# A fused decoder layer on one Trainium2 core: the second norm between the adaLN bursts, and small products stacked in the rounded format

## The chip, the cores and the metric

The kernel runs on one core of one Trainium2 chip. The metric is the device time of one execution in microseconds (us). The engines are named as in the profile: PE (TensorE matmul) with PEld (its weight loads), DVE (VectorE), ACT (ScalarE), POOL (GpSimd) and SP (SyncE, which issues most weight loads).

## The reference

One layer of a hybrid decoder is computed for two groups that share all weights: a prompt of 256 tokens and 8 sample sequences of 8 tokens, 320 token columns together. Everything is float32.

```python
mod = silu(c) @ w_ada + b_ada;  sh1, sc1, g1, sh2, sc2, g2 = split(mod, 6)
h = rmsnorm(x, norm1_g) * (1 + sc1) + sh1
q, k, v, og, u, ga, gb, alr = split(h @ w_in)            # alr: rank 16
loga = log_sigmoid(alr @ w_a2 + b_a) / 16                # gate logits
o, s_new = gla(q, k, v, loga, s0)                        # 4 heads, chunks of 16 tokens, masked
y_a = rmsnorm(o, gla_norm_g) * silu(og);  y_b = pool(u)
x = x + g1 * ((sigmoid(ga) * y_a + sigmoid(gb) * y_b) @ w_o)
h2 = rmsnorm(x, norm2_g) * (1 + sc2) + sh2
gate, up = split(h2 @ w_gu)
x = x + g2 * ((silu(gate) * up) @ w_down)
```

Model width is 2048, FFN width 5632, head sizes 256 (keys) and 512 (values). Outputs are the final normed tokens, the GLA states and the pooling buffers.

## The kernel before

Activations lie transposed, 128 features by 320 tokens a tile, 16 tiles for the model width. Weights stream from HBM in chunks of 0.5 MB. PE has a rounded format of float32 (fp32r), and each projection is built from three such products: a weight chunk is split by ACT into its rounded part whi (L147) and by DVE into the rest wlo (L148), activations are split in the same way into a high and a low tile (hh/hl after the first norm, mh/ml before w_o, h2h/h2l after the second norm), and `mm3` (L161 to L163) adds whi with high, whi with low and wlo with high. whi and wlo have four buffers each (WB = 4, 512 columns a buffer).

The order is: the first adaLN sections and norm; then, head by head, the projections of w_in (units q, k, u, v, og, ga, gb) with steps of GLA and of the pooling branch laid between them; then w_o (with the residual and the squares for each feature tile, L937 to L971); the second norm (L973 to L996); the FFN in two parts of 22 tiles each. A tile scheduler moves instructions within what dependences, buffers and its own estimate of times allow, so that the order on an engine isn't that of the code.

What the change touches:

- `alr_proj` (L462 to L479), once: the low-rank gate input. Two chunks of eight feature tiles; weights of 16 columns sit in 64-column tiles wal (whi and wlo kept apart), with three matmuls per feature tile, 48 in all.
- In `gla_steps`, one call a head: `s_wa2` (L540 to L544) loads w_a2 and b_a on POOL's queue; `s_gk` (L546 on) makes the gate logits by three full float32 matmuls (L549). `s_attP` computes the masked products of keys and queries of the sample sequences (four sequences of eight tokens to a 128 x 128 tile, two tiles gg), and `s_inter(gg)` multiplies them by the sample values vp, in full float32 (L736), and adds the product with the carried state (L740). The sample key tile keP holds two copies of its rows; the values vp stacked by rows serve the state update (L761) in the rounded format as well.
- `ada_burst` (L267 on): adaLN for the second half of the layer is computed in 30 bursts, each a group of matmuls (L279) on a piece of w_ada that `ada_load` and `ada_piece` have loaded (L255, POOL's queue). Bursts 24 and 25 (eight feature tiles each) finish the first half of section 5 (g2), 26 to 29 (four each) the second half. When a half is finished, its sums are copied from PSUM to adasb (ACT L286), transposed by PE (L125) and added to mod (DVE L291).
- At the second norm: bursts 24 and 25 and the norm's sum over partitions (L975) stand behind the last w_o matmul; from it come the root (ACT L977), the reciprocal (DVE L978), the products h (DVE L989, for the sample columns POOL L990 and L991), h2h (ACT L992, L993) and h2l (DVE L994, L996). The first unit of the FFN takes gate and up together. Bursts 26 to 29 stand in the FFN at f = 4, 8, 12 and 16.

Of the kernel before, what the change touches and what calls it, by code (L numbers as in the profile page):

```python
# [11 lines left out]
F32 = mybir.dt.float32  # L12
F32R = mybir.dt.float32r
# [7 lines left out]
P = 128  # L21
# [20 lines left out]
def shape_constants():  # L42
    s = np.arange(P)[:, None]
    c = np.arange(P)[None, :]
    m = 32 * (c // 32) + 15
    dq = ((s > m) & (s <= c)).astype(np.float32) - ((s > c) & (s <= m)).astype(np.float32)
    e = np.zeros((P, 4, 4), np.float32)
    for j in range(4):
        for i in range(j + 1, 4):
            sv = np.arange(P)  # L50
            e[:, j, i] = (sv > 32 * j + 15) & (sv <= 32 * i + 15)
    e = e.reshape(P, 16)
    after = (s > c).astype(np.float32)
# [12 lines left out]
    cf = np.concatenate([inv.reshape(P, 64), m0, m1, ms], 1).astype(np.float32)  # L66
    mask = (s <= c).astype(np.int32)
    r = np.arange(P)[:, None]
    q = np.arange(P)[None, :]
    mp = ((r // 32 == q // 32) & ((r % 32) < 16) & ((q % 32) < 8)  # L70
          & ((r % 8) <= (q % 32))).astype(np.int32)
# [5 lines left out]
CFW = NM0 + NM1 + NMS + 64  # L77


def body(tc, A):  # L80
# [22 lines left out]

    cst = cp.tile([P, 2 * P + 64], F32, name="cst")
# [4 lines left out]
    invc = cst[:, 2 * P:2 * P + 64]  # L109
    cumr = cp.tile([P, NM0 + NM1 + NMS], F32R, name="cumr")  # L110
    M0, M1, MS = cumr[:, 0:NM0], cumr[:, NM0:NM0 + NM1], cumr[:, NM0 + NM1:NM0 + NM1 + NMS]
# [8 lines left out]
    N1G, N2G, FG, PSC, GNG = vec[:, 0:16], vec[:, 16:32], vec[:, 32:48], vec[:, 48:64], vec[:, 64:68]  # L120
    alr = cp.tile([P, 3 * P], F32, name="alr")

# [119 lines left out]
    BURSTS += [(5, 0, 0, 8), (5, 0, 8, 8)] + [(5, NBA, k0, 4) for k0 in range(0, KT, 4)]  # L242
    AMIX, AEND = 24, 26
    ada_raw = {}
    ada_done = []
    ada_want = []
    ada_ps = []

    def ada_piece(after=None):
# [7 lines left out]
    def ada_load(n, bufs):  # L257

        if n < len(BURSTS) and n not in ada_raw:
            nk = BURSTS[n][3]  # L260
            t = ada_raw[n] = apool[0].tile([P, nk, NBA * P], F32, tag="big", bufs=bufs, name=nm("araw"))
            ada_want.extend((n, t, r) for r in range(0, nk, 2))
# [5 lines left out]
    def ada_burst():  # L268
# [7 lines left out]
        with tc.high_priority(), tc.issue_after(last_mm[0]):  # L276
            for r in range(nk):
                for j in range(4):
                    PE.matmul(ps[32 * j:32 * j + 32, 0:2 * P], lhsT=scT[:, k0 + r, :],  # L279
                              rhs=ada_raw[n][:, r, 2 * j * P:(2 * j + 2) * P],  # L280
                              start=k0 + r == 0, stop=k0 + r == KT - 1, tile_position=(0, 32 * j))
        if k0 + nk < KT:
# [109 lines left out]
    with tc.tile_pool(name="head", bufs=1) as xp:  # L392
# [69 lines left out]
        def alr_proj(walr, cum):  # L462
            V.tensor_copy(cumr, cum)
            pa = misc()
            for k0 in range(0, KT, 8):
                wal = []
                for tag in ("whi", "wlo"):
                    t = wp.tile([P, 8, 64], F32R, tag=tag, bufs=WB, name=nm("wal"))
                    G.memset(t.bitcast(F32), 0.0)
                    wal.append(t)  # L470
                wk = walr[:, k0:k0 + 8]
                S.copy(wal[0][:, :, 0:16], wk)
                V.tensor_sub(wal[1][:, :, 0:16], wk, wal[0][:, :, 0:16].bitcast(F32))
                for j in range(8):
                    k = k0 + j
                    mm3(pa[:64, 0:T], wal[0][:, j], wal[1][:, j], hh[k], hl[k], k == 0, k == KT - 1)
            G.memset(alr, 0.0)
            G.memset(alr[32:33, :], 1.0)
            V.tensor_copy(alr[0:16, 0:T], pa[0:16, 0:T])  # L479

        g0 = new_group(0)
        new_gates(g0)
        for si, (k0, k1) in enumerate(SLICES):
# [10 lines left out]
            elif si == len(SLICES) - 1:  # L494
# [3 lines left out]
                cum = xp.tile([P, NM0 + NM1 + NMS], F32, name="cum")  # L498
                nc.gpsimd.dma_start(cum, A["cf"][:, 64:CFW])
                nc.gpsimd.dma_start(invc, A["cf"][:, 0:64])  # L500
            us = units(0)
# [33 lines left out]
    def gla_steps(g):  # L535
# [4 lines left out]
        def s_wa2():  # L540
            wa2 = E["wa2"] = w4([P, DK])
            G.memset(wa2, 0.0)
            nc.gpsimd.dma_start(wa2[0:16, :], A["w_a2"][0, :, DK * h:DK * h + DK])
            nc.gpsimd.dma_start(wa2[32:33, :], A["b_a"][:, DK * h:DK * h + DK])  # L544

# [41 lines left out]
        def s_prod():  # L587
# [145 lines left out]
        def s_inter(gg):  # L733
            def f():
                pt = E["oi"] = misc()
                PE.matmul(pt, lhsT=attP[:, gg], rhs=E["vp"][:, gg].bitcast(F32), start=True, stop=False,  # L736
                          skip_group_check=True)
# [220 lines left out]

    ada_load(AMIX, 2)
    ada_load(AMIX + 1, 2)  # L960
    for ui in range(8):
# [11 lines left out]
    def rstd_bcast(acc):  # L973
        pt = misc()
        PE.matmul(pt[:, 0:T], lhsT=ones, rhs=acc, start=True, stop=True)  # L975
        rs = fp.tile([P, T], F32, tag="rs", name=nm("rs"))
# [5 lines left out]
    ada_burst()  # L982
    rs = rstd_bcast(acc)
    ada_burst()
    h2h = [hp.tile([P, T], F32R, tag="hh%d" % k, name="h2h%d" % k) for k in range(KT)]
# [20 lines left out]
    for pi, (f0, f1) in enumerate(parts):  # L1006
        ah, al = {}, {}
        for f in range(f0, f1, 2):
            sg = fa.tile([P, 2, T], F32, tag="sg", name=nm("sg"))
            if f == 0:  # L1010
                pg, pu = projs(((wgu, f * P), (wgu, FF + f * P)), 0, KT, h2h, h2l)
                S.activation(sg, pg[:, :, 0:T], AF.Silu)
# [10 lines left out]
            if pi == 0 and f >= 2:  # L1023
                if f in (4, 8, 12, 16):
                    ada_burst()
                if f in (2, 4, 8, 12):
                    ada_load(len(ada_done), 1)
                    ada_all()
# [70 lines left out]
```

## Time and profile before

| | |
|---|---|
| time, median of 3 runs | 1989.35 us (1987.7 to 1989.87) |
| profiled execution | 1987.48 us |
| its span | 1985.2 us |
| mean granted TensorE clock | 0.996 |
| busy: PE, PEld | 97%, 91% |
| busy: DVE, ACT, POOL | 50%, 41%, 9% |
| moved by DMA | 400.59 MB, mean 202 GB/s |

The span is the profiled part of one execution. A matmul's record shows when it starts and how long it is under way; in a steady stream the next starts before the last one's record ends, so the cost of a matmul is read from one start to the next. A full float32 matmul shows as two rows. "<-" in a row stands between the written and the read tiles, and a bracket at the end of a row gives the idle time of the engine ahead of it and what ended it.

### The profile page before, as it was taken

What the parts mean: (1) busy time and instruction counts of PE and PEld (TensorE: products, weight loads), DVE (VectorE), ACT (ScalarE), POOL (GpSimd) and SP (SyncE); (2) the same over time, 40 slices, a digit from 0 to 9 for tenths busy, and PEclk for the clock granted to TensorE, in tenths of its full rate; (3) what the DMA queues carried; (4) which work ended last, traced back from release to release, by engine and by line L of the source; (5) the groups of instructions that cost most, each with busy time, mean ns of one, the idle gap of its engine ahead of it and who ended that gap; (6) DMA issues with size and microseconds to landing.
All of it is one profiled execution on the core that took longest, in us unless ns stands there. A gap on an engine that the chain in (4) does not pass through costs nothing.

```text
span 1985.2 us, 34772 instructions
## 1 busy us (share of the span) xinstructions
PE 1934.8 (97%) x13888; PEld 1816.4 (91%) x13888; DVE 998.8 (50%) x1895; ACT 821.7 (41%) x1459; POOL 170.1 (9%) x292
## 2 busy tenths in 40 slices
PE   5999999999999999999999999999999999999997
PEld 3778998988898889989989999999999999999997
DVE  2655645655355535664565444444444444444554
ACT  3323633643345333553444333333333434344443
POOL 1002102211111111111130000000000000000000
PEclk9999999999999999999999999999999999999998
DMA  9997458659865777479745555444444444444443
GB/s 317 349 332 245 133 170 283 231 191 326 292 193 185 277 270 246 147 251 328 271 139 160 184 189 178 155 145 144 156 147 151 149 154 151 150 149 141 148 142 101
DMA packets 309275, 400.59 MB, mean 202 GB/s; under 512 B 12417, under 2 KB 273057, under 8 KB 308777
## 3 DMA queue, kind: packets, MB, share of 16 engines
q1 hardware_dynamic: 279754, 291.17, 45.8%
q0 software_dynamic: 29360, 107.21, 14.7%
q8 instruction: 108, 1.77, 0.4%
q14 instruction: 53, 0.43, 0.1%
HBM read 373.90 MB, written 24.67 MB: 201 GB/s over the span
## 4 chain that ended last, share of the span: by engine, by line
PE 75%; DMA 2%; issue 1%; POOL 1%; ACT 0%; DVE 0%; ACTq 0%; POOLq 0%
PE ps L161 23%; PE ps L163 23%; PE ps L162 23%; PE pm L279 3%; DMA araw<-w_ada 2%; PE pm L125 1%; PE pm L740 0%; PE pm L761 0%; PE pm L709 0%; DMA o_gs<-S 0%; PE pm L736 0%; POOL og L382 0%; PE pm L698 0%; PE psy L161 0%; PE pm L575 0%
## 5 line engine op out<-in xcount | busy, mean ns | idle before, releaser
L148 DVE TENSOR_TENSOR wlo<-raw,whi 128x512 fp32r<-128x512 f32 x952 | 655.2, 692 | 785.9 <-ACT whi L147 780.4
L147 ACT CAST whi<-raw 128x512 fp32r<-128x512 f32 x952 | 586.2, 622 | 940.1 <-PE ps L162 860.9
L161 PE MATMUL ps<-hh,whi 128*128 128x320 f32 x1408 | 442.5, 315 | 2.2 <-ACT whi L147 1.1
L161 PE MATMUL ps<-h2h,whi 128*128 128x320 f32 x1408 | 435.5, 309 | 4.9 <-ACT h2h L993 4.9
L162 PE MATMUL ps<-hl,whi 128*128 128x320 f32 x1408 | 439.1, 312 | 0.0
L163 PE MATMUL ps<-hh,wlo 128*128 128x320 f32 x1408 | 436.6, 313 | 1.4 <-DVE wlo L148 1.3
L162 PE MATMUL ps<-h2l,whi 128*128 128x320 f32 x1408 | 435.0, 309 | 0.0
L163 PE MATMUL ps<-h2h,wlo 128*128 128x320 f32 x1408 | 434.7, 309 | 0.0
L161 PEld LDWEIGHTS ps<-hh,whi 128*128 128x128 f32 x1408 | 264.3, 188 | 25.0 <-issue 13.3
L163 PEld LDWEIGHTS ps<-hh,wlo 128*128 128x128 f32 x1408 | 263.6, 188 | 17.6 <-issue 8.6
L162 PEld LDWEIGHTS ps<-hl,whi 128*128 128x128 f32 x1408 | 264.5, 188 | 7.5 <-issue 6.4
L161 PEld LDWEIGHTS ps<-h2h,whi 128*128 128x128 f32 x1408 | 264.9, 188 | 6.8 <-ACT h2h L993 5.2
L162 PEld LDWEIGHTS ps<-h2l,whi 128*128 128x128 f32 x1408 | 264.8, 188 | 0.0
L163 PEld LDWEIGHTS ps<-h2h,wlo 128*128 128x128 f32 x1408 | 264.7, 188 | 0.1
L161 PE MATMUL ps<-ah,whi 128*128 128x320 f32 x704 | 217.7, 309 | 0.0
L162 PE MATMUL ps<-al,whi 128*128 128x320 f32 x704 | 216.5, 308 | 0.0
L163 PE MATMUL ps<-ah,wlo 128*128 128x320 f32 x704 | 216.5, 308 | 0.0
L162 PEld LDWEIGHTS ps<-al,whi 128*128 128x128 f32 x704 | 131.9, 187 | 0.0
L161 PEld LDWEIGHTS ps<-ah,whi 128*128 128x128 f32 x704 | 131.9, 187 | 0.0
L163 PEld LDWEIGHTS ps<-ah,wlo 128*128 128x128 f32 x704 | 131.9, 187 | 0.0
L255 POOL DMA_DIRECT2D araw<-w_ada x64 | 45.9, 719 | 441.5 <-PE pm L279 423.3
L163 PE MATMUL ps<-mh,wlo 128*128 128x320 f32 x256 | 79.6, 311 | 0.0
(279 smaller groups left out, 1580.9 us busy)
## 6 DMA issues: line engine op xcount, KB each, us to landing
raw<-w_gu SPq DMA_DIRECT2D x176, 512.0 KB, 3.5
raw<-w_in SPq DMA_DIRECT2D x173, 512.0 KB, 4.3
araw<-w_ada POOLq DMA_DIRECT2D x64, 1024.0 KB, 7.7
raw<-w_down SPq DMA_DIRECT2D x80, 512.0 KB, 3.4
raw<-w_ada SPq DMA_DIRECT2D x64, 512.0 KB, 6.9
S<-state_gla POOLq DMA_DIRECT2D x16, 1024.0 KB, 9.1
o_gs<-S POOLq DMA_DIRECT2D x16, 1024.0 KB, 5.8
raw<-w_o SPq DMA_DIRECT2D x32, 512.0 KB, 4.9
```

Of the source, the lines that this page charges most:

```text
L125: PE.transpose(out, in_, ident[:k, :k])
L147: S.copy(hi, raw)
L148: V.tensor_sub(lo, raw, hi.bitcast(F32))
L161: PE.matmul(ps, lhsT=whi, rhs=xhi, start=start, stop=False)
L162: PE.matmul(ps, lhsT=whi, rhs=xlo, start=False, stop=False)
L163: last_mm[:] = [PE.matmul(ps, lhsT=wlo, rhs=xhi, start=False, stop=stop).ins]
L255: nc.gpsimd.dma_start(t[:, r:r + 2], wada[:, k0 + r:k0 + r + 2, col:col + NBA * P])
L279: PE.matmul(ps[32 * j:32 * j + 32, 0:2 * P], lhsT=scT[:, k0 + r, :], rhs=ada_raw[n][:, r, 2 * j * P:(2 * j + 2) * P], start=k0 + r == 0, s ...
```

## The change

Four parts of the kernel change:

1. The weights of the low-rank projection are stacked in one 128-column tile: rounded part and rest in 32 columns, three times. Two matmuls per feature tile (with hh and with hl) give all products at once, 32 in all. `alr` becomes a tile in the rounded format whose rows hold high and low parts, by one subtraction with a column of minus ones and zeros (TAKE_A).
2. `s_wa2` loads six copies of w_a2 and two of b_a and splits them by rows in the same way (an ACT cast and a DVE scalar_tensor_tensor), so the three matmuls of `s_gk` are in the rounded format.
3. keP holds four copies, the mask keeps the rows of the copies, and a cast and a scalar_tensor_tensor turn attP into attR, whose rows hold high and low parts; `s_inter` uses it in the rounded format.
4. The norm's sum over partitions stands between bursts 24 and 25, burst 26 follows, and the first FFN unit is issued behind the last matmul of burst 26. Burst 26 is loaded during w_o, and the FFN keeps the bursts 27 to 29, at f = 4, 8 and 12.

The core of the diff:

```diff
-            for k0 in range(0, KT, 8):
...
-                    mm3(pa[:64, 0:T], wal[0][:, j], wal[1][:, j], hh[k], hl[k], k == 0, k == KT - 1)
-            G.memset(alr, 0.0)
-            G.memset(alr[32:33, :], 1.0)
-            V.tensor_copy(alr[0:16, 0:T], pa[0:16, 0:T])
+            for k0 in range(0, KT, 4):
+                t = wp.tile([P, 4, P], F32R, tag="whi", bufs=WB, name=nm("wal"))
+                G.memset(t[:, :, 96:P].bitcast(F32), 0.0)
+                wk = walr[:, k0:k0 + 4]
+                S.copy(t[:, :, 0:16], wk)
+                V.tensor_sub(t[:, :, 16:32], wk, t[:, :, 0:16].bitcast(F32))
+                G.tensor_copy(t[:, :, 32:64], t[:, :, 0:32].bitcast(F32))
+                G.tensor_copy(t[:, :, 64:96], t[:, :, 0:32].bitcast(F32))
+                for j in range(4):
+                    k = k0 + j
+                    PE.matmul(pa[:, 0:T], lhsT=t[:, j], rhs=hh[k], start=k == 0, stop=False)
+                    PE.matmul(pa[:, 0:T], lhsT=t[:, j], rhs=hl[k], start=False, stop=k == KT - 1)
+            ah_ = xp.tile([P, T], F32R, name="alrh")
+            S.copy(ah_, pa[:, 0:T])
+            V.scalar_tensor_tensor(alr[:, 0:T], ah_.bitcast(F32), TAKE_A, pa[:, 0:T], op0=ALU.mult, op1=ALU.add)
...
         def s_wa2():
-            wa2 = E["wa2"] = w4([P, DK])
-            G.memset(wa2, 0.0)
-            nc.gpsimd.dma_start(wa2[0:16, :], A["w_a2"][0, :, DK * h:DK * h + DK])
-            nc.gpsimd.dma_start(wa2[32:33, :], A["b_a"][:, DK * h:DK * h + DK])
+            raw = w4([P, DK])
+            G.memset(raw, 0.0)
+            for r in range(0, 96, 16):
+                nc.gpsimd.dma_start(raw[r:r + 16, :], A["w_a2"][0, :, DK * h:DK * h + DK])
+            for r in (96, 97):
+                nc.gpsimd.dma_start(raw[r:r + 1, :], A["b_a"][:, DK * h:DK * h + DK])
+            hi = w4([P, DK], F32R)
+            S.copy(hi, raw)
+            wa2 = E["wa2"] = w4([P, DK], F32R)
+            V.scalar_tensor_tensor(wa2, hi.bitcast(F32), TAKE_W, raw, op0=ALU.mult, op1=ALU.add)
...
+                G.tensor_copy(keP[:, d, :, 2 * LS:4 * LS], keP[:, d, :, 0:2 * LS])
...
+            hi = w4([P, 2, P], F32R)
+            S.copy(hi, attP)
+            E["attR"] = lp.tile([P, 2, P], F32R, tag="attR", name=nm("attR"))
+            V.scalar_tensor_tensor(E["attR"], hi.bitcast(F32), TAKE_T, attP, op0=ALU.mult, op1=ALU.add)
...
-                PE.matmul(pt, lhsT=attP[:, gg], rhs=E["vp"][:, gg].bitcast(F32), start=True, stop=False,
+                PE.matmul(pt, lhsT=E["attR"][:, gg], rhs=E["vp"][:, gg], start=True, stop=False,
...
-    ada_load(AMIX, 2)
-    ada_load(AMIX + 1, 2)
+    for n in range(AMIX, AMIX + 3):
+        ada_load(n, 2)
...
-        PE.matmul(pt[:, 0:T], lhsT=ones, rhs=acc, start=True, stop=True)
+        last_mm[:] = [PE.matmul(pt[:, 0:T], lhsT=ones, rhs=acc, start=True, stop=True).ins]
...
     ada_burst()
     rs = rstd_bcast(acc)
+    ada_burst()
     ada_burst()
...
-                pg, pu = projs(((wgu, f * P), (wgu, FF + f * P)), 0, KT, h2h, h2l)
+                with tc.issue_after(last_ada[0]):
+                    pg, pu = projs(((wgu, f * P), (wgu, FF + f * P)), 0, KT, h2h, h2l)
...
-                if f in (4, 8, 12, 16):
+                if f in (4, 8, 12):
                     ada_burst()
-                if f in (2, 4, 8, 12):
+                if f in (2, 4, 8):
```

What the scheduler makes of it is seen in the order of the instructions on each engine. PE at the second norm, before: the last w_o matmul (ps, mh), the two bursts (araw), the sum over partitions (acc) and the transposes (adasb), then the first gate unit.

```order
L163 MATMUL ps_10614<-mh_9440,wlo_10738 128x320
L279 MATMUL pm_10769<-araw_9520,scT 32x256 x32
L279 MATMUL pm_10769<-araw_9521,scT 32x256 x32
L975 MATMUL pm_10802<-acc_9517,cst 128x320
L125 MATMUL pm_10839<-cst,adasb_10840 128x128 x2
L161 MATMUL ps_11014<-h2h_10845,whi_11018 128x320
```

The same place after the change (lines are those of the changed kernel):

```order
L167 MATMUL ps_10679<-mh_9502,wlo_10803 128x320
L284 MATMUL pm_10834<-araw_9582,scT 32x256 x32
L993 MATMUL pm_10867<-acc_9579,cst 128x320
L284 MATMUL pm_10834<-araw_9583,scT 32x256 x32
L129 MATMUL pm_10904<-cst,adasb_10905 128x128
L284 MATMUL pm_10910<-araw_9584,scT 32x256 x16
L129 MATMUL pm_10904<-cst,adasb_10905 128x128
L165 MATMUL ps_11096<-h2h_10927,whi_11100 128x320
```

The sum over partitions moved ahead of the second burst, and a third burst stands between the two transposes, ahead of the first gate matmul.

ACT at the same place, before: the last squares, the copy of the burst's sums, the root, then the high parts h2h of 256 prompt columns and 64 sample columns.

```order
L940 ACTIVATE sq_10765<-x_15_9516 128x320
L286 COPY adasb_10840<-pm_10769 128x256
L977 ACTIVATE rs_10804<-pm_10802,epst 128x320
L992 ACTIVATE h2h_10845<-h_1755_10877,mod 128x256
L992 ACTIVATE h2h_10846<-h_1756_10885,mod 128x256
L993 CAST h2h_10845<-h_1755_10877 128x64
```

And after the change:

```order
L958 ACTIVATE sq_10830<-x_15_9578 128x320
L995 ACTIVATE rs_10869<-pm_10867,epst 128x320
L1011 ACTIVATE h2h_10927<-h_1773_10959,mod 128x256
L1011 ACTIVATE h2h_10928<-h_1774_10967,mod 128x256
L1012 CAST h2h_10927<-h_1773_10959 128x64
L291 COPY adasb_10905<-pm_10834 128x256
L1011 ACTIVATE h2h_10929<-h_1775_10975,mod 128x256
```

The copy to adasb moved from ahead of the root to behind the first cast of 64 sample columns.

POOL in the first head after the change, with what each instruction waits for (DMASW0 to DMASW7 are the eight lanes of its DMA queue): the loads of `s_wa2`, between a clearing of the raw tile and a product of the og gate. Before, one load of w_a and one of b_a stood there.

```order
L549 MEMSET w_455_2689 128x256
L823 MEMSET u_2760 128x2x15 [waits DVE_49,Pool_49]
L551 DMA w_455_2689<-w_a 16x256 [waits DMASW4_49,Pool_49]
L551 DMA w_455_2689<-w_a 16x256 [waits DMASW5_49]
L551 DMA w_455_2689<-w_a 16x256 [waits DMASW6_49]
L551 DMA w_455_2689<-w_a 16x256 [waits DMASW7_49]
L551 DMA w_455_2689<-w_a 16x256 [waits DMASW0_49]
L551 DMA w_455_2689<-w_a 16x256 [waits DMASW1_49]
L553 DMA w_455_2689<-b_a 1x16x16 [waits DMASW2_49]
L553 DMA w_455_2689<-b_a 1x16x16 [waits DMASW3_49]
L387 TENSOR_TENSOR og_264<-og_264,sg_3005 128x640 [waits Activation_49]
```

The two loads became eight, each behind the transfer that its lane carried last.

PE in the last head, where the sum over partitions of the head's norm (acc) stands; before, among projections over hh:

```order
L161 MATMUL ps_9217<-hh_87,whi_9236 128x320
L162 MATMUL ps_9217<-hl_103,whi_9236 128x320
L777 MATMUL pm_8452<-acc_8445,cst 128x320
L279 MATMUL pm_8881<-araw_7942,scT 32x256 x16
L163 MATMUL ps_9217<-hh_87,wlo_9237 128x320
```

After the change it stands among the products of the pooling branch (psy), with 16 of them still to come:

```order
L165 MATMUL psy_9439<-dh_8178,whi_9459 128x320
L166 MATMUL psy_9439<-dl_8179,whi_9459 128x320
L795 MATMUL pm_8514<-acc_8507,cst 128x320
L284 MATMUL pm_8943<-araw_7988,scT 32x256 x16
L165 MATMUL psy_9440<-dh_8178,whi_9443 128x320
```

It moved from a place with 82 projection matmuls over hh and 24 of psy behind it in the head to one behind which the products for w_o follow soon.

More of the change, by code (lines that the diff above doesn't have):

```diff
@@ L65, in shape_constants @@
         inv[:, g] = (1.0 / np.minimum(np.arange(16) + 1, w).astype(np.float32))[None]
-    cf = np.concatenate([inv.reshape(P, 64), m0, m1, ms], 1).astype(np.float32)
+    r = np.arange(P)
+    take = -1.0 * np.stack([(r // 32 == 2) | (r == 97), r // 32 == 1, r % 32 >= 16], 1)
+    cf = np.concatenate([inv.reshape(P, 64), take, m0, m1, ms], 1).astype(np.float32)
     mask = (s <= c).astype(np.int32)
@@ L69, in shape_constants @@
     q = np.arange(P)[None, :]
-    mp = ((r // 32 == q // 32) & ((r % 32) < 16) & ((q % 32) < 8)
+    mp = ((r // 32 == q // 32) & ((q % 32) < 8)
           & ((r % 8) <= (q % 32))).astype(np.int32)
@@ L76 @@
 NM0, NM1, NMS = 272, 400, 128
-CFW = NM0 + NM1 + NMS + 64
+CFC = 64 + 3
+CFW = NM0 + NM1 + NMS + CFC
 def body(tc, A):
@@ L101, in body @@
     V, S, G, PE = nc.vector, nc.scalar, nc.gpsimd, nc.tensor
-    cst = cp.tile([P, 2 * P + 64], F32, name="cst")
+    cst = cp.tile([P, 2 * P + CFC], F32, name="cst")
     msk = cp.tile([P, 2 * P], I32, name="msk")
@@ L109, in body @@
     invc = cst[:, 2 * P:2 * P + 64]
+    TAKE_W, TAKE_A, TAKE_T = (cst[:, 2 * P + 64 + i:2 * P + 65 + i] for i in range(3))
     cumr = cp.tile([P, NM0 + NM1 + NMS], F32R, name="cumr")
@@ L120, in body @@
     N1G, N2G, FG, PSC, GNG = vec[:, 0:16], vec[:, 16:32], vec[:, 32:48], vec[:, 48:64], vec[:, 64:68]
-    alr = cp.tile([P, 3 * P], F32, name="alr")
+    alr = cp.tile([P, 3 * P], F32R, name="alr")
     def tr(out, in_):
@@ L242, in body @@
     BURSTS += [(5, 0, 0, 8), (5, 0, 8, 8)] + [(5, NBA, k0, 4) for k0 in range(0, KT, 4)]
-    AMIX, AEND = 24, 26
+    AMIX = 24
     ada_raw = {}
@@ L247, in body @@
     ada_ps = []
+    last_ada = []
     def ada_piece(after=None):
@@ L260, in ada_load @@
             nk = BURSTS[n][3]
-            t = ada_raw[n] = apool[0].tile([P, nk, NBA * P], F32, tag="big", bufs=bufs, name=nm("araw"))
+            t = ada_raw[n] = apool[0].tile([P, nk, NBA * P], F32, tag="big" if nk == 4 else "big2", bufs=bufs if nk == 8 else 1, name=nm("araw"))
             ada_want.extend((n, t, r) for r in range(0, nk, 2))
@@ L278, in ada_burst @@
                 for j in range(4):
-                    PE.matmul(ps[32 * j:32 * j + 32, 0:2 * P], lhsT=scT[:, k0 + r, :],
-                              rhs=ada_raw[n][:, r, 2 * j * P:(2 * j + 2) * P],
-                              start=k0 + r == 0, stop=k0 + r == KT - 1, tile_position=(0, 32 * j))
+                    last_ada[:] = [PE.matmul(ps[32 * j:32 * j + 32, 0:2 * P], lhsT=scT[:, k0 + r, :],
+                                             rhs=ada_raw[n][:, r, 2 * j * P:(2 * j + 2) * P],
+                                             start=k0 + r == 0, stop=k0 + r == KT - 1, tile_position=(0, 32 * j)).ins]
         if k0 + nk < KT:
@@ L464, in alr_proj @@
             pa = misc()
-            for k0 in range(0, KT, 8):
[L466 to L474, printed above, removed]
-                    k = k0 + j
-                    mm3(pa[:64, 0:T], wal[0][:, j], wal[1][:, j], hh[k], hl[k], k == 0, k == KT - 1)
-            G.memset(alr, 0.0)
-            G.memset(alr[32:33, :], 1.0)
-            V.tensor_copy(alr[0:16, 0:T], pa[0:16, 0:T])
+            for k0 in range(0, KT, 4):
[7 more added lines that the diff above has]
+                for j in range(4):
+                    k = k0 + j
+                    PE.matmul(pa[:, 0:T], lhsT=t[:, j], rhs=hh[k], start=k == 0, stop=False)
[3 more added lines that the diff above has]
+            V.scalar_tensor_tensor(alr[:, 0:T], ah_.bitcast(F32), TAKE_A, pa[:, 0:T], op0=ALU.mult, op1=ALU.add)
+            G.memset(alr[:, T:3 * P].bitcast(F32), 0.0)
+            G.memset(alr[96:98, :].bitcast(F32), 1.0)
         g0 = new_group(0)
@@ L498, in body @@
                 cum = xp.tile([P, NM0 + NM1 + NMS], F32, name="cum")
-                nc.gpsimd.dma_start(cum, A["cf"][:, 64:CFW])
-                nc.gpsimd.dma_start(invc, A["cf"][:, 0:64])
+                nc.gpsimd.dma_start(cum, A["cf"][:, CFC:CFW])
+                nc.gpsimd.dma_start(cst[:, 2 * P:], A["cf"][:, 0:CFC])
             us = units(0)
```

## The prediction

> **What bounds the kernel now.** I read the head of the page first, then the costliest groups with the idle time in front of them, then the timeline of TensorE (PE) where the edits sit.
>
> ```profile
> span 1985.2 us, 34772 instructions
> PE 1934.8 (97%) x13888; PEld 1816.4 (91%) x13888; DVE 998.8 (50%) x1895; ACT 821.7 (41%) x1459; POOL 170.1 (9%) x292
> L161 PE MATMUL ps<-hh,whi 128*128 128x320 f32 x1408 | 442.5, 315 | 2.2 <-ACT whi L147 1.1
> L161 PE MATMUL ps<-h2h,whi 128*128 128x320 f32 x1408 | 435.5, 309 | 4.9 <-ACT h2h L993 4.9
> ```
>
> PE is busy for 97% of the span; DVE and ACT for half of it or less. The projections over hh wait 2.2 us in all, those over h2h once, 4.9 us at the second norm. So a microsecond of PE work that goes is a microsecond of time, unless PE then waits for something that was hidden until now. The mean of 315 ns isn't a price, since the records overlap; starts are:
>
> ```profile
> 1299.71 0.31 PE L162 MATMUL ps<-h2l,whi 128*128 128x320 f32 x1
> ...
> 1301.91 0.31 PE L162 MATMUL ps<-h2l,whi 128*128 128x320 f32 x1
> ```
>
> Fifteen starts lie between these two rows, so one matmul in the rounded format over 320 columns costs 2.20/15 = **0.147 us** of PE.
>
> **The change, part by part.**
>
> *Low-rank gate projection.*
>
> ```profile
> L161 PE MATMUL pm<-hh,wal x16: 302/307/308, 178.7 to 186.7; 128*64 128x320 f32 x16
> L162 PE MATMUL pm<-hl,wal x16: 305/309/313, 178.9 to 186.9; 128*64 128x320 f32 x16
> L163 PE MATMUL pm<-hh,wal x16: 304/307/310, 180.5 to 187.0; 128*64 128x320 f32 x16
> L469 POOL MEMSET wal<- x4: 525/526/527, 175.0 to 177.2; 128x512 f32 x4
> ```
>
> 48 matmuls of 320 columns become 32. A wider weight tile (128 columns for 64) leaves the 320 streamed columns as they are, and the projections beside them use 128-wide weights at 0.147. 16 x 0.147 = **-2.35 us**. The added casts and copies (ACT, DVE, POOL) lie beside projection matmuls. No row shows a POOL copy of 128x4x32; the nearest is the clearing of 128x512 in 0.53, with four times the elements. Two copies of at most that length stand in front of each chunk of eight matmuls (1.2 us): 0 to +0.5 us for the first chunk, nothing for the next, which are made meanwhile. I take 0.
>
> *Gate logits (s_gk), one call a head.*
>
> ```profile
> 208.75 1.46 PE L549 MATMUL pm<-w,alr 128*128 128x256 f32 x6
> 209.85 0.50 PE L161 MATMUL ps<-hh,whi 128*128 128x320 f32 x1
> 210.19 0.31 PE L162 MATMUL ps<-hl,whi 128*128 128x320 f32 x1
> ```
>
> The three unrounded matmuls show as six rows: each runs as two passes. They put 210.19 - 208.75 - 0.147 (the L161 between) = 1.29 us into the stream. Three rounded ones of 256 columns aren't in the trace; the nearest rows are 0.147 for 320 columns and 0.23 for 512 (below). Along that line 256 columns cost 0.12; a matmul of 320 columns is the upper end, so three cost 0.35 to 0.44. I take 0.35: 4 heads x 0.94 = **-3.8 us**.
>
> *Sample attention product (s_inter), eight calls.*
>
> ```profile
> 853.94 1.02 PE L736 MATMUL pm<-vp,attP 128*128 128x512 f32 x2
> ...
> 854.94 0.31 PE L163 MATMUL ps<-hh,wlo 128*128 128x320 f32 x1
> ...
> 302.25 0.39 PE L761 MATMUL pm<-vp,w 128*128 128x512 f32 x1
> 302.48 0.31 PE L163 MATMUL ps<-hh,wlo 128*128 128x320 f32 x1
> ```
>
> One projection matmul lies between the first two rows, so the old product takes 1.00 - 0.15 = 0.85 us; the state update L761 streams the same 512 columns in the rounded format in 0.23. 8 x 0.62 = **-5.0 us**. What is new on the other engines is a cast and a scalar_tensor_tensor in each head for attR, the same two for w_a2, and two POOL copies. ACT and DVE have half of their time free; the question is only where these stand in the queue (rivals).
>
> *One adaLN burst less in the FFN (four quarters there become three; the first moves to the norm).*
>
> ```profile
> 1111.41 0.31 PE L163 MATMUL ps<-h2h,wlo 128*128 128x320 f32 x1
> 1111.65 1.93 PE L279 MATMUL pm<-araw,scT 128*32 128x256 f32 x32
> ...
> 1113.77 0.31 PE L162 MATMUL ps<-h2l,whi 128*128 128x320 f32 x1
> ```
>
> Two projection matmuls lie in these 2.36 us, so the burst costs 2.07: **-2.1 us** here. What it costs at the norm is in the next sum.
>
> *The second norm.*
>
> ```profile
> 1012.35 7.11 PE L279 MATMUL pm<-araw,scT 128*32 128x256 f32 x128
> 1019.39 0.81 PE L975 MATMUL pm<-acc,cst 128*128 128x320 f32 x2
> 1020.03 0.38 PE L125 MATMUL pm<-cst,adasb 128*128 128x128 f32 x2
> 1025.33 0.78 PE L161 MATMUL ps<-h2h,whi 128*128 128x320 f32 x2 [4.92 <-ACT h2h L993]
> ...
> 1028.85 0.34 PE L161 MATMUL ps<-h2h,whi 128*128 128x320 f32 x1
> ```
> ```profile
> 1014.86 1.09 DVE L941 TENSOR_TENSOR acc<-acc,sq 128x320 f32<-128x320 f32 x2 [0.40 <-ACT sq L940]
> ...
> 1020.80 2.15 DVE L978 RECIPROCAL rs<-rs 128x320 f32<-128x320 f32 x1
> ```
> ```profile
> 1019.53 0.37 ACT L286 COPY adasb<-pm 128x256 f32<-128x256 f32 x1 [4.33 <-PE pm L279]
> ...
> 1025.04 0.24 ACT L993 CAST h2h<-h 128x64 fp32r<-128x64 f32 x1 [0.56 <-POOL h L991]
> ```
>
> Before, both bursts of eight stand ahead of the norm's sums of squares: 128 rows in 7.04 us, 3.52 for each burst. The squares are done at 1014.86 + 1.09 = 1015.95, so that matmul could start 3.4 us earlier. After the change one burst ends at 1012.35 + 3.52 = 1015.87, the norm matmul starts at 1016.0, and its chain (square root, reciprocal, the sample columns on POOL, their cast on ACT) moves up by 3.39 us: the cast that releases the gates runs 1021.65 to 1021.89. But the order of ACT after the change puts the copy of the second burst's sums (adasb) behind this cast, and PE needs that copy for a transpose that stands ahead of the third burst and of the gates. So: copy until 1022.26, a transpose 0.2 (0.38 for two), the third burst 32 rows at 7.04/128 = 1.76, a transpose 0.2: the first gate matmul at about 1024.5 rather than 1025.33, **-0.8 us**. The second burst ends at about 1016.0 + 0.64 (from the norm matmul to the next row) + 3.52 = 1020.2, so PE is idle for 2.1 us instead of 4.92.
>
> The second part is the clock:
>
> ```profile
> 1026.00:1028.00 2.00, 2.00 (x9) 2.00 (x8) 2.00 (x7) 1.02 (x4) 1.69 (x4) 0.50 1.00 414
> 1970.00:1972.00 2.00, 0.06 (x1) 0.07 (x2) 1.56 (x7) 1.04 (x3) 0.00 (x0) 1.00 0.00 0
> ```
> ```profile
> 1971.94 0.55 PE L125 MATMUL pm<-cst,xg 128*128 128x128 f32 x3 [2.32 <-ACT xg L1046]
> ```
>
> The next to last three figures are the granted clock, the DMA share and GB/s. After the idle 4.92 us the clock was 0.50, and thirteen gate matmuls took 1028.85 - 1025.33 = 3.52 us instead of 13 x 0.147 = 1.91. At 1970 PE was idle for 2.32 us up to 1971.94, and the clock stayed at 1.00. With an idle 2.1 us I expect no loss: **-1.6 us**. From the rows the limit lies somewhere between 2.32 and 4.92 us. The Trainium skill, "TensorE: Matmul & The Clock Gate" (Part 1: The HAM clock gate), has a free-running window of about 3.4 us, which halves the clock when the array was idle all through it. By that rule 2.1 us never fills a window, and the third burst ahead of the gates would take up a late clock change besides.
>
> Norm in all -2.4. **Sum: 2.35 + 3.8 + 5.0 + 2.1 + 2.4 = 15.6 us.** The profiled execution took 1987.48 us (2.3 around its span of 1985.2); 1987.48 - 15.6 = 1971.9. The median of the runs, 1989.35, lies 1.9 above the profiled execution, so on its footing the forecast is **1973.8 us**. 0.2%, about what a measurement of this kernel can tell from no change, is 4.0 us.
>
> **The rivals.**
>
> *The norm gives nothing.* If POOL, DVE or ACT make the chain 1.3 us or more later than I worked out, PE's idle time comes to 3.4 us or more, well into the stretch between 2.32 and 4.92 that no row decides. Then the gates start no sooner than before and cold, and the third burst may run cold too (twice 1.76, so 1.8 more): 13.2 - 1.8 = 11.4 to 13.2 us saved, 1976.2 to 1978. For it: the queue order on ACT, by which PE waits on POOL through a copy that has nothing to do with POOL. Against it: POOL no longer issues the two loads below ahead of its first product.
>
> ```profile
> 1020.97 1.47 POOL L255 DMA_DIRECT2D araw<-w_ada  x2 [6.01 <-ACT rs L977]
> ```
>
> *Eight small loads hold ACT in each head.*
>
> ```profile
> L543 POOL DMA_DIRECT2D w<-w_a x4: 512/526/540, 198.1 to 787.2; - x4
> ...
> DMA to landing us min/median/max: 2.0/3.0/4.6
> ```
> ```profile
> L549 PE MATMUL pm<-w,alr x24: 377/379/379, 208.7 to 799.3; 128*128 128x256 f32 x24
> ```
> ```profile
> 207.04 0.62 ACT L147 CAST whi<-raw 128x512 fp32r<-128x512 f32 x1 [1.14 <-PE ps L162]
> 208.80 0.62 ACT L147 CAST whi<-raw 128x512 fp32r<-128x512 f32 x1 [1.14 <-PE ps L162]
> ```
>
> Before, two loads per head were waited for by PE alone, 208.7 - 198.1 = 10.6 us after the issue in head 0, 12 in head 3. Now the cast waits for the last of eight, 8 x 0.526 + 3.0 = 7.2 us after the first issue (up to 8.8 with the longest landing), and the weight casts queue behind it on ACT, the weight subtractions behind its partner on DVE. ACT casts a chunk every 1.76 us and waits for PE to free one of four buffers, so it is three chunks ahead, 3 x 1.76 - 0.62 = 4.7 us of cover. If the order was planned with instant loads, PE loses 7.2 - 4.7 = 2.5 to 4.1 us a head, 10 to 16 in all; at 3 us a head the time is 1973.8 + 12 = 1985.8, no change. Against it: the issues stand well ahead of the cast, and ACT and DVE catch up between heads. In the order each of the eight issues waits for a DMA lane of its own, not for the one before it. If they went one by one all the same, 8 x 3.0 = 24 us, a cast as near to its load as PE's use is now (10.6 us) would hold ACT for 13.4, 8.7 of them beyond the cover, 35 us in four heads: 2009, the slow end, which I give 0.02. The Trainium skill, "DMA: Bandwidth & Descriptors" (Anatomy of one DMA), gives a load about 2 us whatever its size, most of it the receipt of the last write; eight in a row would be 16 us by an estimate from that page, against 24 by the row.
>
> *The last head's norm comes late (slower).*
>
> ```profile
> 872.92 0.70 PE L777 MATMUL pm<-acc,cst 128*128 128x320 f32 x2
> ```
> ```profile
> 882.58 0.48 DVE L875 TENSOR_TENSOR EQK<-EQK,og 128x320 f32<-128x320 f32 x1
> ```
>
> From the last head's norm matmul to its last product are 883.06 - 872.92 = 10.1 us; merge, cast and subtraction for w_o add about 5. Before, 82 projection matmuls over hh, 24 of psy and the first of w_o stood behind it, over 20 us of work. In the new order 16 psy, 72 w_o matmuls and two bursts stand behind it before the products are needed: 88 x 0.147 + 2 x 2.07 = 17 us against 15, 2 us of cover. Each microsecond beyond costs one. To end slower than before by 0.2% the chain would have to come 2 + 15.6 + 4 = 22 us late: only if DVE, where the reciprocal now stands ahead of weight subtractions, is held by a second wait. A loss of 1 to 3 us is far likelier than that, and the range has it.
>
> *The rounded products don't come cheaper.* If s_gk and s_inter still went in two passes, 8.8 us of the sum are gone: 1982.6. Against it: L549 and L736 show two rows for a matmul, L761 one, and the new operands have L761's format.
>
> **How the numbers follow.** Forecast 0.66 (1970 to 1978 with the bounds of the unknown costs: 0.5 for the low-rank part, 0.4 for s_gk, up to 3 for the last head, -2 if the copy of adasb comes early); no gain at the norm 0.14; ACT held 0.10; slower 0.05 (last head 0.03, loads one by one 0.02); not cheaper 0.05. The range 1970 to 1983 holds the first two and the last, 0.85, and leaves out the other two. Faster by over 0.2% (below 1985.4): 0.66 + 0.14 + 0.05 and a third of the ACT case, 0.88; within 0.2%: the rest of that case, 0.07; slower 0.05.
>
> **What would show it.** 32 rows of wal rather than 48; three rows of s_gk per head, adding 0.35 us to the stream; one row for each sample product, adding 0.23; three bursts after 1030. At the norm: the sums of squares 3.4 us sooner after the last w_o matmul, an idle time of about 2 us ahead of a transpose rather than 4.92 ahead of the gates, and a granted clock of 1.00 behind it. Wrong would be: an idle time on PE in each head put down to a weight cast on ACT (loads), one near the end of the fourth head with mh as its operand (last head), or a clock of 0.50 in the first gates.

## The result, and the profile after

| | before | after |
|---|---|---|
| time, median (6 runs each) | 1988.51 us (1986.08 to 1989.87) | 1976.57 us (1975.08 to 1978.53) |
| profiled execution | 1987.48 us | 1978.01 us |
| its span | 1985.2 us | 1976.2 us |

The ratio is 0.9947, 95% interval 0.9937 to 0.9957: 10.5 us faster by the ratio, 11.9 by the medians, where 15.6 were forecast. The time lies in the range; 4 to 5 us of the gain are missing. The time alone would also fit the rival that the norm gives nothing (1976.2 to 1978), so the terms have to be read from the traces. The head of the page of after, then its costliest groups:

```profile
span 1976.2 us, 34764 instructions
PE 1927.1 (98%) x13852; PEld 1812.4 (92%) x13852; DVE 1005.3 (51%) x1905; ACT 822.5 (42%) x1469; POOL 184.7 (9%) x332
L165 PE MATMUL ps<-hh,whi 128*128 128x320 f32 x1408 | 442.5, 315 | 2.8 <-ACT whi L151 2.1
L165 PE MATMUL ps<-h2h,whi 128*128 128x320 f32 x1408 | 434.6, 309 | 0.0
```

The busy time of PE went down by 7.7 us and the 4.9 us of idle time ahead of the gates are gone. The projections over hh wait 0.6 us more than before, and the next group, the projections of w_o, which read mh, has a wait on a weight cast that the page of before does not list:

```profile
L165 PE MATMUL ps<-mh,whi 128*128 128x320 f32 x256 | 80.2, 313 | 3.0 <-ACT whi L151 2.2
```

Now the places that the prediction named. PE in the timeline of after, a sample product, then a gate-logit step (columns: start, duration, instruction, idle time ahead):

```profile
436.67 0.40 PE L754 MATMUL pm<-vp,attR 128*128 128x512 f32 x1
436.91 0.30 PE L166 MATMUL ps<-hl,whi 128*128 128x320 f32 x1
...
594.36 0.52 PE L562 MATMUL pm<-w,alr 128*128 128x256 f32 x3
594.71 0.31 PE L165 MATMUL ps<-hh,whi 128*128 128x320 f32 x1
```

From start to start, a sample product takes 0.24 us and three gate-logit matmuls 0.35. The low-rank projection has 32 rows (16 for L480, 16 for L481). The second norm on PE:

```profile
1006.95 0.31 PE L167 MATMUL ps<-mh,wlo 128*128 128x320 f32 x1
1007.19 3.66 PE L284 MATMUL pm<-araw,scT 128*32 128x256 f32 x64
1010.85 0.81 PE L993 MATMUL pm<-acc,cst 128*128 128x320 f32 x2
1011.58 3.66 PE L284 MATMUL pm<-araw,scT 128*32 128x256 f32 x64
1017.15 0.33 PE L129 MATMUL pm<-cst,adasb 128*128 128x128 f32 x1 [1.91 <-ACT adasb L291]
1017.41 1.93 PE L284 MATMUL pm<-araw,scT 128*32 128x256 f32 x32
1019.28 0.33 PE L129 MATMUL pm<-cst,adasb 128*128 128x128 f32 x1
1019.36 0.39 PE L165 MATMUL ps<-h2h,whi 128*128 128x320 f32 x1
```

The sums of squares stand between the two bursts, and the idle time is 1.91 us ahead of a transpose. The clock stays at full speed (windows of 2 us of after, the third figure from the end):

```profile
1018.00:1020.00 2.00, 2.00 (x33) 1.25 (x23) 2.00 (x7) 1.20 (x4) 1.84 (x6) 1.00 0.03 8
1020.00:1022.00 2.00, 2.00 (x16) 2.00 (x15) 2.00 (x8) 1.12 (x4) 1.98 (x4) 1.00 0.28 53
```

**Where the time went.** For each matmul that both traces have I took its start in after less its start in before:

| place | after less before, us | step |
|---|---|---|
| first projection over hh | +0.5 | +0.5 |
| first w_o matmul | -12.5 | -13.0: -11.15 products as worked out, about -2.4 for two half-bursts (16 matmuls of w_ada each) that are now issued in w_o, +0.6 left over for other waits and the slow clock in head 0 |
| end of w_o | -5.2 | **+7.3**: about 2.4 the half-bursts, 4.9 lost |
| first gate matmul | -6.0 | -0.8 |
| behind the thirteen first gate matmuls | -7.6 | -1.66 (clock) |
| after the FFN's bursts | -9.7 | -2.1 |
| end of the span | -9.0 | +0.7 (the half clock of the tail sets in sooner) |

All terms of the sum are there. What is missing is lost in w_o, a stage where the prediction had costed nothing. PE and ACT there, in the timeline of after:

```profile
946.68 0.31 PE L167 MATMUL ps<-mh,wlo 128*128 128x320 f32 x1
949.15 0.63 PE L165 MATMUL ps<-mh,whi 128*128 128x320 f32 x1 [2.16 <-ACT whi L151]
```
```profile
936.38 0.62 ACT L151 CAST whi<-raw 128x512 fp32r<-128x512 f32 x1 [0.46 <-PE ps L166]
942.01 1.14 ACT L151 CAST whi<-raw 128x512 fp32r<-128x512 f32 x2 [5.01 <-DMA raw<-w_o]
948.48 1.14 ACT L151 CAST whi<-raw 128x512 fp32r<-128x512 f32 x2 [5.33 <-DMA raw<-w_o]
```

Twice ACT's cast waits over 5 us for a chunk of w_o from HBM; behind the second wait PE stands for 2.16 us. The windows of after over this stretch (the last three figures are granted clock, DMA share, GB/s):

```profile
940.00:942.00 2.00, 2.00 (x16) 2.00 (x15) 0.00 (x0) 0.00 (x0) 0.00 (x0) 1.00 1.05 397
...
946.00:948.00 2.00, 0.99 (x7) 0.72 (x5) 0.00 (x0) 0.00 (x0) 0.00 (x0) 1.00 1.05 404
...
950.00:952.00 2.00, 2.00 (x9) 2.00 (x9) 1.74 (x7) 0.36 (x1) 0.30 (x2) 0.50 1.10 348
```

The DMA engines are busy all the time, and behind the wait the clock is halved. Of the 4.9 us, 0.83 are a wait of a burst for its load near 902, 2.16 this wait, and some 1.7 the slow clock. POOL, in the timeline of after, shows what else was moved (each araw piece is 1 MB):

```profile
918.23 0.55 POOL L985 TENSOR_TENSOR xs<-x,mod 128x64 f32<-128x64 f32 x2 [8.31 <-DVE x L966]
927.09 2.89 POOL L260 DMA_DIRECT2D araw<-w_ada  x4 [8.32 <-PE pm L129]
```

Four pieces go out together at 927 and two more near 936, and the chunks of w_o issued between 928 and 942 land late (run 6 shows how late). POOL had stood still for 8.3 us ahead of them: the buffer of burst 24, in a pool that part 4 makes 16 KB larger, comes free only with the transposes that follow burst 23.

### The profile page after: what moved, and what is told of

It reads as the page before. It is cut to its first block, busy times and chain, and to the rows that moved or that the text cites. A ratio compares the mean times of both kernels' runs of the same rounds, so it can differ in the third digit from the quotient of the medians.

```text
span 1976.2 us, 34764 instructions
## 1 busy us (share of the span) xinstructions
PE 1927.1 (98%) x13852; PEld 1812.4 (92%) x13852; DVE 1005.3 (51%) x1905; ACT 822.5 (42%) x1469; POOL 184.7 (9%) x332
## 3 DMA queue, kind: packets, MB, share of 16 engines
q8 instruction: 108, 1.77, 0.4%
## 4 chain that ended last, share of the span: by engine, by line
PE 82%; DMA 2%; ACT 1%; DVE 1%; issue 0%; POOL 0%; ACTq 0%; DVEq 0%; POOLq 0%
PE ps L167 25%; PE ps L165 25%; PE ps L166 25%; PE pm L284 3%; PE pm L129 1%; DMA araw<-w_ada 1%; PE pm L779 1%; PE pm L758 1%; PE pm L723 1%; DMA raw<-w_o 1%; DMA raw<-w_in 1%; PE pm L712 0%; DVE wlo L152 0%; PE pm L653 0%; ACT whi L151 0%
## 5 line engine op out<-in xcount | busy, mean ns | idle before, releaser
L165 PE MATMUL ps<-mh,whi 128*128 128x320 f32 x256 | 80.2, 313 | 3.0 <-ACT whi L151 2.2
```

The lines of the kernel that those rows point to most:

```text
L165: PE.matmul(ps, lhsT=whi, rhs=xhi, start=start, stop=False)
```

## The experiments

The letters in the expectations are theories on the missing time. **A**: the hold of POOL at 918 to 927 costs it, by the place of the buffers. **V** (A'): the volume of w_ada in the w_o stage does. **B**: ACT's queue in head 0. **N** (C): no cause that lies in the loads, such as the spread between executions. **D**, formed after the first four runs: w_o is bound by its transfers, and once PE comes there 12 us sooner, w_ada pieces issued early in it push its own chunks back. Kernels that ran together share the runs of before. Gains and losses in us are the ratio's distance from 1 times the median of before.

**1. Burst 26 in a pool of its own**, which ends the hold (e1_pool_apart).

```diff
-    for n in range(AMIX, AMIX + 3):
+    for n in range(AMIX, AMIX + 2):
         ada_load(n, 2)
+    aw = apool[0]
+    apool[0] = wcx.enter_context(tc.tile_pool(name="aw2", bufs=1))
+    ada_load(AMIX + 2, 1)
+    apool[0] = aw
```

> The changed kernel, with burst 26's tile in a small pool of its own, so that the big tiles of bursts 24 and 25 lie where they lay before; the same ten loads of 1 MB in the w_o stage. Theory A (the place: with the 16 KB more, the load of burst 24 waits for the transposes of burst 23, POOL stands from 918.8 to 927.1 us, six loads then fall into 10 us, the weight chunks come late, PE idles 0.83 and 2.16 us and its clock is halved once): the stalls of w_o go, 4.9 us less than the changed kernel, about -16 us against before. Rival A' (the volume: 2 MB more in the w_o stage): w_o keeps its stalls, -12 us against before as the changed kernel. Rival C (one unlucky profile, no steady cause): -12 us, and stalls in other places.

Measured: 1987.07 us beside 1986.90 of before, 0.9997 (0.9988 to 1.0005). The whole gain is gone. Without the hold burst 24's pieces go out at once, and ACT in the timeline of this kernel shows a far longer wait:

```profile
922.08 1.14 ACT L151 CAST whi<-raw 128x512 fp32r<-128x512 f32 x2 [14.46 <-DMA raw<-w_o]
```

PE loses 7.5 us there in one wait, 2.3 in three others and more by the clock. A falls as the whole cause: without the hold w_o loses far more than with it. What the hold leaves is the bunch of six pieces behind it, and with that the 2.16 us of after.

**2. After without the third burst at the norm** (e2_two_bursts): burst 26 goes back to the FFN, with the old pool.

```diff
-    for n in range(AMIX, AMIX + 3):
-        ada_load(n, 2)
+    ada_load(AMIX, 2)
+    ada_load(AMIX + 1, 2)
...
     ada_burst()
-    ada_burst()
...
-                if f in (4, 8, 12):
+                if f in (4, 8, 12, 16):
```

> The changed kernel without the third burst at the norm: its load and its matmuls are back in the FFN (four bursts there), the norm's sum still between bursts 24 and 25. Theories A and A' alike: no stalls in w_o (-4.9 us), gates start 1.9 us sooner, the burst costs 2.1 us in the FFN again: about -16.5 us against before. Rival B (the shortfall lies in the heads): -12 us. If the gates' clock drops after the idle time ahead of them, 1.6 us more.

Measured: 1986.46 us, 0.9996 (0.9987 to 1.0004), not the -16.5 us expected, with a wait of 7.0 us in w_o. Fewer loads in the whole stage, but more of them early: V, as a matter of the stage's total, falls too.

**3. Parts 1 to 3 alone** (e3_products_alone): before, with the three product edits.

> Before with the stacked products only (parts 1 to 3), the norm as before. By the prediction's terms -11.15 us. Theory A: the w_o stage is as before, so -11 us, less what ACT's queue in head 0 costs (rival B: a wait of 2.1 us and a halved clock near 242 us, some 2 us net): -9 to -11 us.

Measured: 1991.18 us, 1.0018 (1.001 to 1.0027), 3.6 us slower where 9 to 11 faster were expected. This kernel is 11.9 us ahead at the first w_o matmul and 5.3 us behind at the end of w_o: 17 us go in that one stage, about 2.4 of them the two half-bursts that moved there and nearly 15 lost. POOL and PE in the timeline of this kernel, and two windows of it:

```profile
902.18 0.76 POOL L259 DMA_DIRECT2D araw<-w_ada  x1 [0.32 <-POOL xs L984]
...
908.61 1.43 POOL L259 DMA_DIRECT2D araw<-w_ada  x2 [4.64 <-PE pm L283]
```
```profile
920.11 0.63 PE L165 MATMUL ps<-mh,whi 128*128 128x320 f32 x1 [7.24 <-ACT whi L151]
```
```profile
900.00:910.00 10.00, 9.57 (x82) 7.95 (x82) 3.34 (x9) 1.98 (x4) 3.45 (x6) 1.00 1.05 386
910.00:920.00 10.00, 2.87 (x20) 2.60 (x18) 0.00 (x0) 0.56 (x2) 0.04 (x1) 0.77 1.04 396
```

With transfers at 396 GB/s, PE works for 2.9 of 10 us. The view of the weight chunks in this kernel between 890 and 925 tells how long a load takes from issue to landing:

```profile
L143 SPq DMA_DIRECT2D raw<-w_o x6: 367/890/2322, 892.0 to 923.8; - x6
...
DMA to landing us min/median/max: 3.3/12.5/22.2
```

In before the longest is 11.8 us in the same stretch, in after 13.1.

**4. Part 4 alone** (e4_norm_alone): before, with the norm between the bursts and the third burst behind it.

> Before with the norm part only (part 4). By the prediction's terms -2.4 at the norm and -2.1 in the FFN, -4.5 us. Theory A or A': the w_o stage gives some or all of it back (the first load of burst 24 waits for PE here too, but only two loads fall together): -4.5 to 0 us. Rival B: -4.5 us in full.

Measured: 1982.11 us, 0.9975 (0.9965 to 0.9985), -5.0 us, beside 4.5 worked out for the norm and the FFN. So part 4 gives its gain by itself, parts 1 to 3 by themselves cost 3.6: together -1.4, and yet the whole change gives -10.5. What makes the difference is the hold, which part 4 brings with it: run 1 has parts 1 to 4 without it and gains nothing.

**5. Parts 1 to 3 with the loads later** (e5_products_loads_late), the test of D: the pieces of w_ada hang behind the feature tiles 4 to 11 of w_o rather than 0 to 7.

```diff
-            if ada_want:
+            if ada_want and k >= 4:
                 ada_piece(gi)
```

> The kernel of e3 (stacked products alone), with the eight loads of bursts 24 and 25 hung behind feature tiles 4 to 11 of w_o instead of 0 to 7. Theory D (the w_o stage is bound by transfers: the PE time saved in the heads brings its start 12 us forward, while the loads of bursts 22 and 23 still come in PE's pace, so that they and the first pieces of burst 24 fall together with the first w_o chunks): the waits of w_o go, and the time is 9 to 11 us under before. Rival V (it is the amount of w_ada that falls into the w_o stage, wherever in it): still over -4 us. Rival N (the loss of e3 has nothing to do with loads): +4 us as e3.

Measured: 1977.26 us beside 1986.74, 0.9955 (0.9941 to 0.9969). One condition turns +3.6 into -8.9 us. No matmul of w_o waits for an ACT cast any more, and the view of the weight chunks of this kernel between 890 and 925 ends with

```profile
DMA to landing us min/median/max: 4.9/8.4/12.8
```

D holds.

**6. After with the same condition** (e6_after_loads_late).

> The changed kernel, with the ten loads of bursts 24 to 26 behind feature tiles 4 to 13 of w_o instead of 0 to 9. Theory D: no wait on weights in w_o, 4.9 us less than the changed kernel, -16 to -17 us against before. Rival V: about -12 us.

Measured: 1974.68 us, 0.9941 (0.9927 to 0.9955): -11.7 us, not the -16 to -17 expected, and by its interval not to be told from after. In the trace the waits for weights in w_o are gone: from its first matmul to its end the lead shrinks from 13.1 to 10.5 us, about the 2.4 of the moved half-bursts. The chunks of w_o issued there land sooner. The view of the weight chunks between 928 and 942 ends, in after and then in this kernel, with

```profile
DMA to landing us min/median/max: 11.3/13.7/14.7
```
```profile
DMA to landing us min/median/max: 3.4/3.6/9.8
```

One wait of 1.5 us is new, where the sums of squares now come later than PE (1007.06, for DVE's acc).

**7. The copy of adasb ahead of the first sample cast** (e7_after_copy_first), on top of 6, with the pool of 1.

```diff
-        S.copy(h2h[k][:, TP:T], t[:, TP:T])
+        with tc.issue_after(last_copy[0]) if k == 0 else nullcontext():
+            S.copy(h2h[k][:, TP:T], t[:, TP:T])
```

> As e6, with burst 26's tile in a pool of its own, and the copy of burst 25's sums on ACT ahead of the first cast of sample columns instead of behind it. By the chain of the norm: the transpose and the third burst run while PE waited, the first gate matmul follows the cast at once, about 2 us sooner: -18 to -19 us against before. Rival: PE's work ahead of the gates is only moved, the cast comes no sooner and the gates start where they did: as e6.

Measured: 1973.26 us, 0.9933 (0.992 to 0.9946): -13.3 us, not the -18 to -19 expected. From the norm's matmul to the first gate it takes 7.60 us, in after 8.51, so 0.9 us come of the 2 expected; PE still waits 1.00 us for the copy (1011.55). The pool of its own, ruinous in 1, does no harm here, since the loads are late.

**8. Before with four loads early** (e8_before_loads_early): the fault of D put into a kernel that doesn't have it.

```diff
     ada_load(AMIX + 1, 2)
+    for _ in range(4):
+        ada_piece()
```

> Before, with the first four pieces of burst 24 issued at the start of the w_o stage rather than one behind each of the tiles 0 to 3: nothing else differs. Theory D: the same pile of transfers as in e3, PE waits for weights: 5 to 17 us slower. Rival N: within 1 us of before.

Measured: 2006.84 us, 1.0103 (1.0088 to 1.0117), +20 us, without any change to a product or a norm. The waits of PE by line, between 885 and 1008, in this kernel:

```profile
PE ps L161 <- ACT whi L147: 12.1, 2, 7.6
```

**9. After once more** (e9_after_again), in the group of the next three.

> The changed kernel itself, beside the others on one chip. Theory D (its w_o stage waits for weights in most executions): about -12 us against before, and its trace shows again waits on weight casts near 945 us in w_o and a halved clock behind them. Rival C (the first profile was an unlucky one): no such wait, and a span some 4 us shorter.

Measured: 1978.14 us beside 1987.31, 0.9951 (0.9938 to 0.9963). The same wait in w_o, 2.24 us at 949.54 behind a cast that waited 5.32 for its chunk, so N falls for that part. At the norm the idle time is 1.92 us, and this time the clock drops; a window of this execution:

```profile
1020.00:1022.00 2.00, 2.00 (x19) 0.98 (x12) 0.97 (x4) 1.24 (x4) 0.85 (x2) 0.50 0.00 0
```

**10. The copy ahead of the 256-column casts as well** (e10_copy_ahead), for k < 2, on top of 7.

> As e7, with the copy of burst 25's sums also ahead of the first two h2h of 256 columns on ACT. By the chain of the norm: the copy starts at the reciprocal's end rather than 0.9 us behind it, the third burst ends before the first cast of sample columns, and the gates start 0.7 to 0.9 us sooner than in e7: -14 to -16 us against before. Rival: the gates then wait for the cast instead, no gain over e7.

Measured: 1972.41 us, 0.9921 (0.9909 to 0.9934), -15.7 us; norm matmul to first gate 7.09 us, idle time ahead of the transpose 0.49.

**11. Head 0's output gates ahead of its exponential** (e11_gates_before_exp), on top of 10. In after, ACT in the timeline of head 0 goes 8 us without a weight cast:

```profile
235.27 0.62 ACT L151 CAST whi<-raw 128x512 fp32r<-128x512 f32 x1 [1.14 <-PE ps L166]
235.79 0.86 ACT L570 ACTIVATE w<-pm 128x512 f32<-128x512 f32 x2
236.55 0.74 ACT L383 ACTIVATE sg<-mg 128x640 f32<-128x640 f32 x1
237.30 1.28 ACT L571 ACT_TABLE_LOAD   x1
238.60 0.85 ACT L571 ACTIVATE w<-w 128x768 f32<-128x768 f32 x1
239.46 1.28 ACT L572 ACT_TABLE_LOAD   x1
240.76 0.94 ACT L572 ACTIVATE w<-w,onet 128x768 f32<-128x768 f32 x1
241.71 1.28 ACT L383 ACT_TABLE_LOAD   x1
243.01 0.74 ACT L383 ACTIVATE sg<-mg 128x640 f32<-128x640 f32 x1
243.65 0.60 ACT L151 CAST whi<-raw 128x512 fp32r<-128x512 f32 x1
```

PE then waits 1.29 us at 244.30 and 0.82 at 245.98. The edit puts both sigmoids (L383) ahead of the exponential (L571):

```diff
-            S.activation(t1, t1, AF.Exp, scale=-1.0)
+            with tc.issue_after(last_sg[0]) if h == 0 else nullcontext():
+                S.activation(t1, t1, AF.Exp, scale=-1.0)
...
-    queue += pst + st[:PSY] + [sig0] + psy + st[PSY:] + [merge_step(g0, E)]
+    queue += [sig0] + pst + st[:PSY] + psy + st[PSY:] + [merge_step(g0, E)]
```

> As e10, and in head 0 both sigmoids of the og gate stand ahead of the exponential of the gate logits on ACT, so that one table load goes and weight casts come between the exponential and the logarithm. Theory B (the waits near 244 and 262 us come from ACT's queue, 8 us without a weight cast against some 4.7 us of cover): the waits of 1.28, 0.82, 0.46 and 0.17 us go, 2.7 us less than e10, -17 to -18 us. Rival: ACT is late there for another reason (PE's or DMA's), waits stay.

Measured: 1970.81 us (1969.35 to 1971.08), 0.9914 (0.99 to 0.9928), the fastest of all: 17.1 us below before, and 7.4 below after by the ratio of run 9 on the same chip. Its interval overlaps that of run 10, so what the edit is worth is read from the trace. The waits at 244 and 246 are gone; some 1.1 us of waits are gained of the 2.7 expected, since a second batch of exponentials and sigmoids between 250 and 258 us keeps a wait of 1.31 us at 259.31.

**12. Before with the loads later** (e12_before_loads_late).

> Before, with the eight loads of bursts 24 and 25 behind tiles 4 to 11 of w_o. Theory D: before has no wait on weights in w_o on PE, so nothing is to be had: within 1 us. Rival (late loads gain by themselves, whatever the products do): -2 to -5 us.

Measured: 1988.05 us, 1.0004 (0.9995 to 1.0013), no change. Late loads bring nothing until the products bring w_o forward.

The runs on w_o in one view: pieces of w_ada issued from 8 us before to 28 us after the first w_o matmul, by POOL's rows, and PE's longest wait there for a weight cast.

| kernel | MB in that time | next pieces | longest wait, us |
|---|---|---|---|
| 12 (before, loads late) | 4 | two at +50 | none |
| before | 6 | two at +35 | none |
| 4 | 6 | two at +36 | 0.9 |
| 5, 6, 7, 10, 11 | 6 | two at +53 | none |
| after, 9 | 6 | four at +44, two by +54 | 2.2 |
| 1, 2, 3 | 8 | | 7.0 to 7.5 |
| 8 | 10 | | 7.6 (12.1 in two) |

The count is a rough measure: counted from 20 us ahead of w_o, before has 8 MB as well, and no wait. The cause is shown by runs 5, 8 and 12, which move the loads and nothing else.

## Why the prediction was right, and where it failed

*Products.* Right: the rows of after have the prices that were worked out, and with 2.35 + 3.8 + 5.0 = 11.15 the drift up to w_o leaves 0.6 us for everything else. 256 rounded columns cost 0.118 us each (0.353/3), the line through 0.147 and 0.23 had given 0.12. The rival that rounded products don't come cheaper is out.

*FFN and norm.* -2.1 and -2.1; -0.8 and -0.8; the clock -1.6 and -1.66. Idle time 2.1 worked out and 1.91 found, behind the copy of adasb, as said; runs 7 and 10 move that copy and take 0.9 and 1.4 us from the stretch. The limit on the clock, put between 2.32 and 4.92 us, did not hold, though: 1.91 us kept full speed in one execution of after, 1.92 us halved it in another. The row it was read from misleads, too: in before the clock was still 1.00 at 1971.94, but it was halved from 1974.40. That the idle time at the norm kept full speed in the first profile was luck (the last section shows why). So this term is 1.66 us in some executions and about nothing in others, and that may be part of the spread of after.

*The step that failed* is the first paragraph's "a microsecond of PE work that goes is a microsecond of time, unless PE then waits for something that was hidden until now", which was never put to w_o. The loads there, burst 26's included, were costed at nothing, with no row of that stage weighed. A window of before shows that its DMA engines were busy all the time already, though no matmul waited (the last two figures are DMA share and GB/s):

```profile
910.00:920.00 10.00, 10.00 (x86) 8.64 (x79) 5.02 (x12) 4.00 (x8) 2.06 (x4) 1.00 1.08 339
```
Coming 12 us sooner, w_o meets w_ada pieces whose times hang on POOL's buffers, and its chunks land late. That takes 4.9 us of after, nearly 15 us of the products alone (run 3), and is undone by delaying the pieces (run 5: -8.9) and brought about without the products by sending them early (run 8: +20). No rival named it. The forecast came near only because part 4's larger pool held POOL back for 8 us, by chance of its buffers: that is luck, since run 1 has every term of the sum without the hold and gains nothing.

*ACT held in each head.* Partly right, with another cause. The eight small loads hold nobody: in head 0 their cast (L555) starts 12 us behind the first issue (215.3 to 227.3), and in no head does ACT stand idle ahead of it. In head 0 the gate logits' exponential and logarithm meet the output gates' sigmoids, and three table loads of 1.28 us make 8 us without a weight cast, against the 4.7 us of cover worked out. PE waits 2.1 us (1.29 + 0.82), and the clock is halved behind it (0.50 from 246 to 248). Waits of before that went away make up for most, so the sum in the heads is +0.6.

*The last head comes late.* Not seen: no matmul waits for the norm's chain. PE waits 0.8 us at the first w_o matmul, for a product of the pooling branch (L885).

*What stays open.* By its trace run 6 should have gained 4 us more than after, and the ratios differ by 0.0006, 1.2 us, with intervals that overlap: that the wait in w_o is gone is shown, that this is worth 4 us in the median is not. Which load delays which chunk was not traced one by one. The wait at 259 us in run 11 was not tried.

## What to carry to other kernels

Work taken from the bound engine ahead of a stage that fills the DMA engines is only kept if the transfers into that stage keep their distance: count the megabytes issued around its start, before and after, by the issuing engine's order of instructions, and read how long its chunks take from issue to landing. A larger pool or an earlier start moves loads that no line of the diff names. A copy or a run of activations from different tables is priced by what stands behind it on its queue, not by its own time.

## What the runs showed of the hardware

- Transfers on POOL's queue slow those on SP's: with 8 MB of w_ada issued in the 36 us around the start of w_o, a 0.5 MB chunk took up to 22.2 us to land, at 396 GB/s in all (run 3), against 12.8 at most in run 5 with 6 MB.
- The clock is not decided by the length of one idle time alone, but in steps of 3.413 us. In each of the 14 traces the granted clock changes only at whole multiples of this from its other changes (in after it is halved from 245.74 and from 948.89, 206 steps apart, for one step each). Behind the first 100 us of these traces, no full-speed step in which PE was idle for less than 1.75 us was followed by half speed, every one with 1.92 us or more was, and between the two it went either way. The 2.32 us in the tail of before fell into two steps, with 1.37 us of idle time in the first and 1.77 in the second, behind which the clock was halved; the 2.16 us in w_o of after put 1.90 into one step, and 1.29 and 0.82 in head 0 together 1.87. The Trainium skill, "TensorE: Matmul & The Clock Gate" (Part 1: The HAM clock gate), asks for a window of about 3.4 us in which the array is idle throughout; the length of the window agrees with these traces, the rest does not: none of these three idle times fills such a window, and the clock was halved behind each.
